# A filter network on half the columns, first weights cast behind the squares, tables through GpSimd's queue

## The chip, the cores and the metric

One NeuronCore of one Trainium2 chip runs the whole kernel. The metric is the time of one execution in device microseconds (us); the kernel before was timed three times: 1154.57, 1156.49 and 1156.57 us, median 1156.49. Engines are named as in the profile: PE (matrix multiply), PEld (its weight loads), DVE (vector), ACT (scalar with function tables), POOL (GpSimd), SP (sync). SP, ACT and POOL also issue DMAs; the instructions of each engine run in the order in which they stand in its queue.

## The reference

An encoder layer on `x` of 1024 rows by 1024 columns, float32. `h` is the RMS norm of `x`, and `proj = h @ w_in` is cut into the inputs of two branches and their gates. The part that matters here is the filter of the Hyena branch, which depends on no row of `x`:

```python
h = rms_norm(x, g_norm[l])
proj = h @ w_in[l]
...
# hyena_filter_spectra: z is (L, 33), a fixed table of times t, cos and -sin
h = jnp.sin(freq_1 * (z @ w_f1 + b_f1))          # 33 -> 64
h = jnp.sin(freq_2 * (h @ w_f2 + b_f2))          # 64 -> 64
k = (h @ w_f3).reshape(L, HY_ORDER, 2, HY_WIDTH) # 64 -> 2 orders x 2 directions x 512
k = k * decay[:, None, None, :]
k_full = jnp.concatenate([k[:, :, 0], k[::-1, :, 1]], axis=0)
return jnp.fft.rfft(k_full.astype(jnp.float32), axis=0)
...
zc = gate * long_conv(zc, k_spec[:, o], hy_bias[l, o])
```

The attention branch, the merge of the two and the output projection follow; the change leaves them as they are.

## The kernel before, in words

Every product in float32 is made of three products of float32r parts: a tile is cast to a high part (ACT), the rest is subtracted (DVE), and PE adds high by high, low by high and high by low. `split` (L138, L139) makes the two parts, `gsplit` (L142, L143) does it with a scale.

**Start.** `load_x` brings `x` in eight tiles of 128 rows, by SP and ACT in turns. `build_hT` works on two groups of four tiles: squares and their sums (ACT, in the first group DVE too), a reciprocal root in twelve tiny DVE instructions (`rsqrt`, L152 to L158), rows scaled on DVE (`xs`, L223), transposes on PE into PSUM (`ptx`, L230), and the two parts of the transposed rows, `hh` on ACT and `hl` on DVE.

**Projection blocks.** `proj_block` loads 128 columns of `w_in` as two `wr` tiles (SP), splits them into `wh` and `wl`, and runs 48 matmuls of 512 columns (`pm`, L567) into two PSUM banks. `fill_g` makes a gate of such a block (ACT, sigmoid) and stores it. `wr` has two buffers: SP issues the next load when DVE has made the `wl` of the tile two before. Eight gate blocks (GEARLY) are written next to the filter stage and fill PE there.

**Filter network.** `filter_loads` brings the table of times `z2` and the two small weights on SP's queue. `z2` holds the 33 features of a time in rows 0 to 32 and those of the mirrored time in rows 64 to 96, for all 1024 times; `wf1` and `wf2` are block diagonal, so one product gives both directions. `filter_mlp` runs each layer on two tiles of 512 columns: three matmuls (`pf`), then `sin_layer` (L254 to L261): scale on DVE (`sx`), two instructions that give the multiple of 2 pi (`sk`), three that subtract it (L258), a clamp, and the sine on ACT. `filter_tables` splits the third layer's weight (`w3h`, `w3l`) and the transform table `ku` (`kuh`, `kul`) on ACT and DVE.

**Spectra.** `filter_spectra` has four rounds (order by half of the channels). In a round, four steps take the third layer's product (`pk`, L348 and L349, two PSUM banks) times the decay (`kk`, L350) into `A` and `B`; the table `dec` of 512 KB for a step comes by SP's queue into one of two buffers, so its load is issued when the step two before has been multiplied. Then `forward` and `leaf_fwd` transform the sums (`pu`, L128) and store the spectra.

Who goes first is decided when the program is built: a scheduler puts the instructions of each engine in one order, with `behind` adding an order without a wait (`after=self.half0` puts the small casts behind the first half of `hh`). On PE the matmuls of projection blocks stand between those of the filter.

The functions that the change touches, with the profile's line numbers:

Of the kernel before, what the change touches and what calls it, by code (L numbers as in the profile page):

```python
# [10 lines left out]
F32 = mybir.dt.float32  # L11
F32R = mybir.dt.float32r
# [29 lines left out]

def _constants():
# [19 lines left out]
    for k in KS[1:]:  # L63
# [24 lines left out]
    return {  # L88
        "sel": sel, "z2": z2, "dec": d2, "ku": ku, "gu": gu, "rt": rt,
        "ident": np.eye(P, dtype=f32),  # L90
    }


class K:
# [106 lines left out]
    def build_hT(self, hp, xp):  # L201
# [5 lines left out]
        xt = self.xt  # L207
        bank = lambda t: self.pp.tile([P, 512], F32, tag=t, bufs={"mm": MMB, "tp": 2, "cv": CVB}[t], name=self.nm("ptx"))
        for g in range(2):
            for i in range(4):  # L210
                tt = 4 * g + i
                sq = xp.tile([P, D], F32, tag="sq", bufs=2, name=self.nm("sq"))
                if i % 2 and g == 0:
                    nc.vector.scalar_tensor_tensor(out=sq, in0=xt[tt], scalar=1.0, in1=xt[tt], op0=ALU.mult, op1=ALU.mult, accum_out=ss[:, tt:tt + 1])
                else:
                    nc.scalar.activation(out=sq, in_=xt[tt], func=AF.Square, accum_out=ss[:, tt:tt + 1])
# [30 lines left out]
    def sin_layer(self, fp, ps, b, fr, cols):  # L247
# [3 lines left out]
        x = fp.tile([P, n], F32, tag="sx", bufs=2, name=self.nm("sx"))  # L251
        k = fp.tile([P, n], F32, tag="sk", bufs=2, name=self.nm("sk"))
# [4 lines left out]
        for c in (6.28125, 0.0019350051879882812, 3.019915981956753e-07):  # L257
# [6 lines left out]
    def filter_loads(self, f1):  # L264
        nc, a = self.nc, self.a
        self.selr = f1.tile([P, P], F32, tag="selr", name="selr")
        nc.sync.dma_start(out=self.selr, in_=a["sel"])
# [4 lines left out]
        self.z2 = f1.tile([P, L], F32, tag="z2", name="z2")  # L272
        nc.sync.dma_start(out=self.z2, in_=a["z2"])

    def filter_mlp(self, fp, f1):
# [22 lines left out]
        for c in range(2):
            sl = slice(c * 512, (c + 1) * 512)
            ps = self.pp.tile([P, 512], F32, tag="cv", bufs=CVB, name=self.nm("pf"))  # L300
            self.mm3(ps, w2h, w2l, h1h[:, sl], h1l[:, sl], True, True)
            x = self.sin_layer(f1, ps, fv[:, 2:3], fv[:, 3:4], 512)
            for d in range(2):
                a_, b_ = slice(64 * d, 64 * d + 64), slice(64 - 64 * d, 128 - 64 * d)
                nc.scalar.copy(out=self.h2[d][a_, sl], in_=x[a_])
                nc.vector.tensor_tensor(out=self.h2[d][b_, sl], in0=x[a_], in1=self.h2[d][a_, sl].bitcast(F32), op=ALU.subtract)

    def filter_tables(self, fp):
        nc, a = self.nc, self.a
        self.kuh = fp.tile([P, 18, P], F32R, tag="kuh", name="kuh")  # L310
        self.kul = fp.tile([P, 18, P], F32R, tag="kul", name="kul")
        with self.pool("fp2") as f2:
            wf3 = f2.tile([P, 2, HY], F32, tag="wf3", name="wf3")
            w3v = a["w_f3"][0].rearrange("k (o d c) -> d k o c", o=2, d=2)
            for d in range(2):
                nc.scalar.dma_start(out=wf3[64 * d:64 * d + 64], in_=w3v[d])
            for d in range(2):
                for s in (slice(0, 64), slice(64, 128)):
                    nc.scalar.copy(out=self.w3h[d][s], in_=wf3[64 * d:64 * d + 64])
                s = slice(64 * d, 64 * d + 64)  # L320
# [944 lines left out]
```

## Time and profile before

| | us |
|---|---|
| median of 3 runs | 1156.49 |
| lowest, highest | 1154.57, 1156.57 |
| the profiled execution's own time | 1155.32 |
| its span in the trace | 1153.4 |
| PE busy | 1099.4 (95%) |
| DVE busy | 893.0 (77%) |
| ACT busy | 589.4 (51%) |
| POOL busy | 107.3 (9%) |

The profiled execution lies 1.2 us below the median and inside the range of the three runs. Matmuls overlap each other in the trace, so PE "busy" means that one is under way. "PEclk" is the granted clock as a share of 2.4 GHz: 1.00 is that, 0.50 is 1.2 GHz. A wait is put down to what ended it.

### The profile page before, as it was taken

Reading aid. Unit: us, or ns where it says so; the run is one execution under the profiler, and the core shown is the slowest. Engines: PE = TensorE matmul, PEld = TensorE weight load, DVE = VectorE, ACT = ScalarE, POOL = GpSimd, SP = SyncE. Lnnn points to the kernel's source line nnn. Section 1 sums busy time; section 2 is a strip of 40 time slices with the busy share of each in tenths; the row PEclk is TensorE's granted clock in tenths of the full one; section 3 lists DMA queues with packets and bytes.
Section 4 is the critical chain, followed back from the end, with each engine's and each line's share of the span. In section 5 each row is a group of like instructions: output and inputs, shape, how many; then the busy total and the mean of one; then the engine's idle time right before and its main releaser. Section 6 shows DMA issues by size and latency. Waiting matters only on the chain.

```text
span 1153.4 us, 15529 instructions
## 1 busy us (share of the span) xinstructions
PE 1099.4 (95%) x5525; PEld 909.7 (79%) x5525; DVE 893.0 (77%) x1631; ACT 589.4 (51%) x1101; POOL 107.3 (9%) x112
## 2 busy tenths in 40 slices
PE   4899999999999999999999999999999999999996
PEld 3678888888888888878887887787888887778874
DVE  6988788698788886778774893789788888478882
ACT  6745555754445434433433852777877776322420
POOL 0000000000000000000000132102200000250353
PEclk9989999999999999999999999899999999999998
DMA  5446444642335334334227557402202001896345
GB/s 212 133 146 198 155 163 174 205 119 65 89 91 147 105 115 128 91 88 127 91 83 233 148 154 248 146 29 74 92 25 77 1 20 50 274 298 217 91 128 182
DMA packets 119221, 150.27 MB, mean 130 GB/s; under 512 B 8548, under 2 KB 82408, under 8 KB 119144
## 3 DMA queue, kind: packets, MB, share of 16 engines
q1 hardware_dynamic: 107688, 120.97, 34.1%
q10 hardware_dynamic: 11456, 28.32, 6.6%
q8 instruction: 43, 0.70, 0.3%
q14 instruction: 34, 0.28, 0.1%
HBM read 101.81 MB, written 47.45 MB: 129 GB/s over the span
## 4 chain that ended last, share of the span: by engine, by line
PE 65%; DVE 14%; DMA 10%; ACT 6%; issue 3%; POOL 1%; SPq 0%; ACTq 0%; POOLq 0%; DVEq 0%
PE pm L567 33%; PE pu L128 8%; PE pt L903 4%; PE pi L128 4%; DMA wor<-in_w_out_dram 3%; PE S L119 2%; PE S L122 2%; PE S L121 2%; ACT pr L889 2%; PE pv L915 2%; PE pv L916 2%; DVE gg L988 1%; DMA out_dram<-xr 1%; DVE mo L139 1%; ACT PTh L138 1%
## 5 line engine op out<-in xcount | busy, mean ns | idle before, releaser
L567 PE MATMUL pm<-hh,wh 128*128 128x512 f32 x656 | 208.6, 393 | 1.8 <-DVE hl L143 0.9
L567 PE MATMUL pm<-hl,wh 128*128 128x512 f32 x656 | 208.9, 393 | 0.0
L567 PE MATMUL pm<-hh,wl 128*128 128x512 f32 x656 | 208.3, 392 | 0.1
L567 PEld LDWEIGHTS pm<-hh,wh 128*128 128x128 f32 x656 | 123.1, 189 | 27.7 <-DVE hl L143 1.1
L567 PEld LDWEIGHTS pm<-hh,wl 128*128 128x128 f32 x656 | 123.2, 188 | 26.0 <-DVE wl L139 0.5
L567 PEld LDWEIGHTS pm<-hl,wh 128*128 128x128 f32 x656 | 123.0, 188 | 25.3
L138 ACT CAST wh<-wr 128x512 fp32r<-128x512 f32 x98 | 60.3, 621 | 158.1 <-PE pm L567 107.7
L138 ACT CAST PTh<-pt 128x512 fp32r<-128x512 f32 x128 | 72.8, 587 | 41.1 <-PE pt L903 39.6
L139 DVE TENSOR_TENSOR PTl<-pt,PTh 128x512 fp32r<-128x512 f32 x128 | 83.8, 682 | 10.8 <-ACT PTh L138 10.2
L887 DVE TENSOR_REDUCE mx<-S 128x1 f32<-128x1024 f32 x64 | 77.9, 1217 | 13.2 <-PE S L122 13.1
L139 DVE TENSOR_TENSOR wl<-wr,wh 128x512 fp32r<-128x512 f32 x95 | 66.8, 708 | 15.7 <-ACT wh L138 15.4
L903 PE MATMUL pt<-ident,pr 128*128 128x128 f32 x512 | 75.9, 278 | 2.4 <-DVE PTl L139 1.4
L889 ACT ACTIVATE pr<-S,mx 128x1024 f32<-128x1024 f32 x64 | 71.8, 1121 | 7.0 <-DVE mx L887 6.6
L903 PEld LDWEIGHTS pt<-ident,pr 128*128 128x128 f32 x512 | 59.3, 142 | 18.2 <-DVE PTl L139 4.7
L915 PE MATMUL pv<-PTh,vc 128*128 128x256 f32 x256 | 69.1, 297 | 0.4 <-DVE at L926 0.4
L916 PE MATMUL pv<-PTl,vc 128*128 128x256 f32 x256 | 67.9, 293 | 0.0
L473 DVE TENSOR_TENSOR t<-pu,kt 128x512 f32<-128x512 f32 x64 | 41.0, 681 | 31.3 <-PE pu L128 30.7
L138 ACT CAST rh<-res 128x512 fp32r<-128x512 f32 x64 | 39.5, 619 | 41.8 <-PE pu L128 20.5
L119 PE MATMUL S<-kh,qh 96*128 96x512 f32 x128 | 54.5, 426 | 2.4 <-ACT pr L889 2.3
L121 PE MATMUL S<-kh,ql 96*128 96x512 f32 x128 | 53.5, 418 | 0.0
L122 PE MATMUL S<-kl,qh 96*128 96x512 f32 x128 | 52.5, 410 | 0.0
L915 PEld LDWEIGHTS pv<-PTh,vc 128*128 128x128 f32 x256 | 48.5, 189 | 4.7 <-DVE at L926 1.9
(285 smaller groups left out, 2391.2 us busy)
## 6 DMA issues: line engine op xcount, KB each, us to landing
wr<-in_w_in_dram SPq DMA_DIRECT2D x82, 256.0 KB, 3.2
wor<-in_w_out_dram SPq DMA_DIRECT2D x36, 256.0 KB, 4.7
dec<-in_dec_dram SPq DMA_DIRECT2D x16, 512.0 KB, 3.6
gT<-ob ACTq DMA_DIRECT2D x16, 512.0 KB, 2.9
gg<-gT SPq DMA_DIRECT2D x16, 512.0 KB, 4.4
kd<-kt ACTq DMA_DIRECT2D x28, 256.0 KB, 2.3
kt<-kd SPq DMA_DIRECT2D x28, 256.0 KB, 2.7
m<-gg ACTq DMA_DIRECT2D x16, 256.0 KB, 4.3
```

The lines of the kernel that those rows point to most:

```text
L119: m = nc.tensor.matmul(out, lhsT=lh, rhs=rh, start=start, stop=False)
L121: nc.tensor.matmul(out, lhsT=ll, rhs=rh, start=False, stop=False)
L122: nc.tensor.matmul(out, lhsT=lh, rhs=rl, start=False, stop=stop)
L128: m = self.nc.tensor.matmul(out, lhsT=x, rhs=y, start=n == 0, stop=n == len(ops) - 1)
L138: self.behind(self.nc.scalar.copy(out=hi, in_=x), after)
L139: (eng or self.nc.vector).tensor_tensor(out=lo, in0=x, in1=hi.bitcast(F32), op=ALU.subtract)
L567: nc.tensor.matmul(ps[c][0:m], lhsT=w[:, i, 0:m], rhs=h[d][:, c * 512:(c + 1) * 512], start=(d == 0 and f == 0), stop=(d == 7 and f == 2))
L887: nc.vector.tensor_reduce(out=mx, in_=ps, axis=AX.X, op=ALU.max, negate=True)
L889: i = nc.scalar.activation(out=pr, in_=ps, func=AF.Exp, bias=mx, accum_out=RS[h // 2][:, qb, h % 2:h % 2 + 1])
L903: nc.tensor.transpose(out=pt[:, i], in_=pr[:, kb * P:(kb + 1) * P], identity=self.ident)
L915: nc.tensor.matmul(pv, lhsT=V[h][:, kb], rhs=hi[:, kb], start=(kb == 0), stop=False)
L916: nc.tensor.matmul(pv, lhsT=V[h][:, kb], rhs=lo[:, kb], start=False, stop=(kb == 7))
```

## The change

- **Network on half the columns.** The table of times has 512 columns: rows 0 to 32 hold the first 512 times, rows 64 to 96 the other 512. Each layer is one tile of 512 columns: three `pf` matmuls and one `sin_layer` in place of two. The mirrored direction is made at the end: `h2` becomes four tiles, and two DVE copies read a tile backwards (`h[:, ::-1]`). The sine's reduction subtracts in two instructions instead of three.
- **Tables come in two parts.** The high and low parts of `z2` and `ku` are made on the host and loaded as float32r; `sel` is loaded as float32r too. The ACT casts and DVE subtractions of `z2`, `ku` and `sel` are gone, and twice the bytes of `ku` are loaded (2.36 MB in all).
- **GpSimd's queue.** The parts of `z2`, `kuh`, `kul`, `sel`, all sixteen `dec` tables and the four bias rows are issued by POOL, in one order. `follow` starts a group of them with a one-element copy: the `z2` parts behind tile 6 of `x`, `kuh`, `kul` and `sel` behind the low part of the second `w3` tile. SP keeps the weights of the projection.
- **Third weight.** `w_f3` is loaded on ACT's queue in four pieces behind `half0`, both directions on all 128 partitions.
- **First block's order.** `gates` replaces `fill_g`: the casts of block 0 stand behind the last of `x`'s squares on ACT, and its subtractions behind the first group's scaled rows on DVE; those of block 1 behind `half0`; the sigmoid of a block is written after the next block's matmuls.
- **Idle transposes.** 36 transposes of raw `x` tiles, into a bank that nobody reads, stand on PE ahead of the first real ones.
- `sq` gets one buffer for ACT and one for DVE in the first group.

```diff
     z2 = np.zeros((P, L // 2), f32)
     z2[:33] = z[:L // 2].T
     z2[64:97] = z[L // 2:].T
...
     for n, x in (("z2", z2), ("ku", ku)):
         t[n + "h"], t[n + "l"] = _parts(x)
...
+        idle = self.pp.tile([P, 512], F32, tag="tp", bufs=2, name="idle")
+        for i in range(4):
+            for j in range(8 if i < 3 else 12):
+                nc.tensor.transpose(out=idle[:, :P], in_=xt[i][:, (j % 8) * P:(j % 8 + 1) * P], identity=self.ident)
...
+    def follow(self, pool, x, moves):
+        nc = self.nc
+        dum = pool.tile([1, 1], F32, tag="fol", bufs=2, name=self.nm("fol"))
+        last = nc.gpsimd.tensor_copy(out=dum, in_=x)
+        for out, in_ in moves:
+            i = nc.gpsimd.dma_start(out=out, in_=in_)
+            self.behind(i, last)
+            last = i
...
+        wf3 = [f1.tile([P, 2, HY], F32, tag=f"wf3{d}", name=f"wf3{d}") for d in range(2)]
+        for d in range(2):
+            for s in range(2):
+                self.behind(nc.scalar.dma_start(out=wf3[d][64 * s:64 * s + 64], in_=w3v[d]), self.half0)
...
+        ps = self.pp.tile([P, L // 2], F32, tag="cv", bufs=CVB, name=self.nm("pf"))
+        self.mm3(ps, w1h, w1l, zh, zl, True, True)
+        x = self.sin_layer(f1, ps, fv[:, 0:1], fv[:, 1:2], L // 2)
+        self.split(x, h1h, h1l)
+        for d in range(2):
+            self.split(wf3[d], self.w3h[d], self.w3l[d], after=self.half0)
+        ps = self.pp.tile([P, L // 2], F32, tag="cv", bufs=CVB, name=self.nm("pf"))
+        self.mm3(ps, w2h, w2l, h1h, h1l, True, True)
+        x = self.sin_layer(f1, ps, fv[:, 2:3], fv[:, 3:4], L // 2)
         for c in range(2):
+            a_, b_ = slice(64 * c, 64 * c + 64), slice(64 - 64 * c, 128 - 64 * c)
+            h, r = self.h2[0, c], self.h2[1, 1 - c]
+            nc.scalar.copy(out=h[a_], in_=x[a_])
+            nc.vector.tensor_tensor(out=h[b_], in0=x[a_], in1=h[a_].bitcast(F32), op=ALU.subtract)
+            nc.vector.tensor_copy(out=r, in_=h[:, ::-1].bitcast(F32))
...
-                    nc.sync.dma_start(out=dec, in_=a["dec"][hf, tp].rearrange("p (d t c) -> p d t c", d=2, t=2))
+                    nc.gpsimd.dma_start(out=dec, in_=a["dec"][hf, tp].rearrange("p (d t c) -> p d t c", d=2, t=2))
+                    if (o, hf, tp) == (0, 0, 1):
+                        self.follow(wk, self.w3l[1][0:1, 0, 0:1].bitcast(F32), ((self.kuh, a["kuh"]), (self.kul, a["kul"]), (self.sel, a["sel"])))
...
+    def gates(self, bs):
+        ps = None
+        for b in bs:
+            new = self.proj_block(3232 + b * P, P, *(((self.squares, self.scaled), (self.half0, None)) + ((None, None),) * 14)[b])
+            if ps is not None:
+                self.gate_out(b - 1, ps)
+            ps = new
+        self.gate_out(bs[-1], ps)
```

How the instructions stand: on DVE, in the first layer of the network. `pf` is a layer's product, `sx` and `sk` its sine's tiles, `wl` a projection weight's low part (`wl_1635` belongs to block 1 before, `wl_1620` and `wl_1650` to block 1 and the next two to block 2 in the change). Before:

```order
L254 TENSOR_SCALAR sx_364<-pf_360,cols 128x512
L139 TENSOR_TENSOR wl_1635<-wr_1632,wh_1634 128x512
L255 TENSOR_SCALAR sk_365<-sx_364 128x512
L254 TENSOR_SCALAR sx_382<-pf_378,cols 128x512
L256 TENSOR_SCALAR sk_365<-sk_365 128x512
L255 TENSOR_SCALAR sk_383<-sx_382 128x512
L258 SCALAR_TENSOR_TENSOR sx_364<-sk_365,sx_364 128x512
L256 TENSOR_SCALAR sk_383<-sk_383 128x512
```

And in the change, from the low part of the third weight on:

```order
L148 TENSOR_TENSOR w3l_384<-wf_390,w3h_382 128x1024
L266 TENSOR_SCALAR sx_410<-pf_406,cols 128x512
L148 TENSOR_TENSOR w3l_385<-wf_391,w3h_383 128x1024
L267 TENSOR_SCALAR sk_411<-sx_410 128x512
L148 TENSOR_TENSOR wl_1620<-wr_1617,wh_1619 128x512
L268 TENSOR_SCALAR sk_411<-sk_411 128x512
L148 TENSOR_TENSOR wl_1650<-wr_1647,wh_1649 128x512
L270 SCALAR_TENSOR_TENSOR sx_410<-sk_411,sx_410 128x512 x2
L272 TENSOR_SCALAR sx_410<-sx_410 128x512
L148 TENSOR_TENSOR wl_1686<-wr_1683,wh_1685 128x512
L148 TENSOR_TENSOR wl_1716<-wr_1713,wh_1715 128x512
L148 TENSOR_TENSOR h1l<-sx_410,h1h 128x512
```

One chain of the sine stands where two stood in turns; the low parts of `w3` now come ahead of block 1's first `wl`, and those of block 2 ahead of `h1l`.

On PE, at the first `pk` of the spectra (third layer; `pm` are projection matmuls: 1630 and 1631 block 1 before, 1681 and 1682 block 2 in the change). Before, `pk` follows the last matmuls of block 1:

```order
L567 MATMUL pm_1630<-hl_154,wh_1664 128x512
L567 MATMUL pm_1631<-hl_154,wh_1664 128x512
L567 MATMUL pm_1630<-hh_146,wl_1665 128x512
L567 MATMUL pm_1631<-hh_146,wl_1665 128x512
L348 MATMUL pk_475<-w3h_340,h_344 128x256
L349 MATMUL pk_475<-w3l_342,h_344 128x256
```

In the change it follows the 33rd matmul of block 2:

```order
L577 MATMUL pm_1681<-hh_148,wl_1716 128x512
L577 MATMUL pm_1682<-hh_148,wl_1716 128x512
L577 MATMUL pm_1681<-hh_149,wh_1715 128x512
L577 MATMUL pm_1682<-hh_149,wh_1715 128x512
L577 MATMUL pm_1681<-hl_157,wh_1715 128x512
L358 MATMUL pk_459<-w3h_382,h_386 128x256
L359 MATMUL pk_459<-w3l_384,h_386 128x256
```

Thirty-three more projection matmuls stand ahead of the third layer.

On the queues that issue `dec`, `bia` (a bias row) and `wr` (projection weights). Before, on SP:

```order
L339 DMA bia_470<-in_hy_bias_dram 1x256
L342 DMA dec_472<-in_dec_dram 128x1024
L342 DMA dec_490<-in_dec_dram 128x1024
L339 DMA bia_744<-in_hy_bias_dram 1x256
L559 DMA wr_1764<-in_w_in_dram 128x4x128
L559 DMA wr_1794<-in_w_in_dram 128x4x128
L342 DMA dec_507<-in_dec_dram 128x1024
```

In the change, on POOL, behind the first two `dec`:

```order
L292 COPY fol_476<-w3l_385 1x1
L294 DMA kuh<-in_kuh_dram 128x2304
L294 DMA kul<-in_kul_dram 128x2304
L294 DMA sel<-in_sel_dram 128x128
L349 DMA dec_496<-in_dec_dram 128x1024
L346 DMA bia_1007<-in_hy_bias_dram 1x16x16
L349 DMA dec_513<-in_dec_dram 128x1024
```

The tables of the transform stand between the second and the third `dec`, and no `wr` stands among them any more. From about the 600th microsecond of the span on, the order on every engine is the same in both kernels.

## Rows read from the trace of the kernel before

**Rows 1.** Windows: busy us (count) by engine, then PEclk, DMA share, GB/s.
```profile
core 0: us, PE busy (x) PEld busy (x) DVE busy (x) ACT busy (x) POOL busy (x), PEclk, DMA share, GB/s
45.00:65.00 20.00, 13.23 (x48) 9.79 (x47) 18.50 (x30) 14.20 (x19) 0.00 (x0) 0.83 0.53 170
65.00:620.00 555.00, 554.61 (x2609) 457.73 (x2608) 439.49 (x869) 254.72 (x504) 1.60 (x24) 1.00 0.41 126
```

**Rows 2.** Windows, the gap and the stretch behind it.
```profile
52.70:58.80 6.10, 0.30 (x2) 0.00 (x0) 6.07 (x9) 5.45 (x8) 0.00 (x0) 0.93 0.36 145
58.80:64.70 5.90, 5.38 (x16) 4.41 (x17) 4.87 (x9) 3.02 (x5) 0.00 (x0) 0.50 0.47 149
```

**Rows 3.** Timeline around the first pk: start, us, engine, line, [idle before <-releaser].
```profile
58.12 2.83 DVE L306 TENSOR_TENSOR h<-sx,h 64x512 fp32r<-64x512 f32 x4
...
58.86 0.58 PE L348 MATMUL pk<-w3h,h 128*128 128x256 f32 x1 [5.86 <-DVE h L306]
```

**Rows 4.** Groups by form, 35 to 62 us, DVE: busy us, mean ns.
```profile
L258 DVE SCALAR_TENSOR_TENSOR sx<-sk,sx 128x512 f32<-128x512 f32 x12 | 7.6, 685 | 0.0
L254 DVE TENSOR_SCALAR sx<-pf,cols 128x512 f32<-128x512 f32 x4 | 3.1, 806 | 0.1
...
L139 DVE TENSOR_TENSOR wl<-wr,wh 128x512 fp32r<-128x512 f32 x4 | 2.7, 688 | 0.4 <-ACT wh L138 0.4
L139 DVE TENSOR_TENSOR kul<-kur,kuh 128x1152 fp32r<-128x1152 f32 x2 | 2.6, 1348 | 0.0
L322 DVE TENSOR_TENSOR w3l<-wf,w3h 64x1024 fp32r<-64x1024 f32 x2 | 2.4, 1215 | 0.0
L255 DVE TENSOR_SCALAR sk<-sx 128x512 f32<-128x512 f32 x4 | 1.6, 420 | 0.0
```

**Rows 5.** Timeline of the start: PE, DVE, ACT's queue.
```profile
15.74 5.52 PE L230 MATMUL ptx<-ident,xs 128*128 128x128 f32 x28 [8.60 <-DVE xs L223]
...
21.36 4.70 DVE L143 SCALAR_TENSOR_TENSOR hl<-ptx,cols,hh 128x512 fp32r<-128x512 f32 x7 [0.48 <-ACT hh L142]
...
28.69 1.47 PE L230 MATMUL ptx<-ident,xs 128*128 128x128 f32 x12
...
30.90 5.35 DVE L143 SCALAR_TENSOR_TENSOR hl<-ptx,cols,hh 128x512 fp32r<-128x512 f32 x8
...
34.65 1.27 ACTq L316 DMA_DIRECT2D wf<-in_w_f_dram  x2
```

**Rows 6.** The chain that ended last: start, us, projection matmuls at full clock.
```profile
74.12 9.09 PE pm L567 x40
```

**Rows 7.** Groups by form, 35 to 62 us, ACT.
```profile
L319 ACT CAST w3h<-wf 64x1024 fp32r<-64x1024 f32 x4 | 4.2, 1051 | 3.0 <-DMA wf<-in_w_f_dram 3.0
...
L683 ACT ACT_TABLE_LOAD x2 | 2.6, 1283 | 0.0
...
L261 ACT ACTIVATE sx<-sx 128x512 f32<-128x512 f32 x4 | 2.4, 626 | 1.1 <-DVE sx L260 1.1
...
L138 ACT CAST wh<-wr 128x512 fp32r<-128x512 f32 x2 | 1.1, 613 | 0.0
```

**Rows 8.** DMA issues of the page: count, KB each, median us to landing.
```profile
wr<-in_w_in_dram SPq DMA_DIRECT2D x82, 256.0 KB, 3.2
```

**Rows 9.** DMA view, 2 to 14 us, while x is loaded.
```profile
DMA packets 1890, 4.66 MB, mean 388 GB/s; under 512 B 204, under 2 KB 831, under 8 KB 1890
```

**Rows 10.** Tile dec, all sixteen loads.
```profile
DMA to landing us min/median/max: 3.5/3.6/6.5
```

**Rows 11.** Timeline of the second round: dec issues, kk of step 3, and first pu.
```profile
104.46 2.73 SPq L342 DMA_DIRECT2D dec<-in_dec_dram  x2
...
108.56 1.27 DVE L350 TENSOR_TENSOR kk<-pk,dec 128x512 f32<-128x512 f32 x2
...
119.72 0.13 DVE L115 COPY dum<-rl 1x1 f32<-1x1 f32 x1
...
119.86 0.28 PE L128 MATMUL pu<-rh,kuh 128*128 128x256 f32 x1
```

More of the change, by code (lines that the diff above doesn't have):

```diff
@@ L87, in _constants @@
     sel[0:64:32, :64] = sel[1:64:32, 64:] = 1.0
[L88 to L91, printed above, removed]
+    t = {"sel": sel, "gu": gu, "dec": d2, "rt": rt, "ident": np.eye(P, dtype=f32)}
+    for n, x in (("z2", z2), ("ku", ku)):
+        t[n + "h"], t[n + "l"] = _parts(x)
+    return t
 class K:
@@ L135, in behind, with split @@
             self.tc.add_manual_dep(i.ins, after.ins.name, mybir.DependencyInfo(mybir.DependencyClass.NoSync, mybir.DependencyReason.DATA), reason="order")
-    def split(self, x, hi, lo, eng=None, after=None):
+    def split(self, x, hi, lo, eng=None, after=None, then=None):
         self.behind(self.nc.scalar.copy(out=hi, in_=x), after)
-        (eng or self.nc.vector).tensor_tensor(out=lo, in0=x, in1=hi.bitcast(F32), op=ALU.subtract)
+        self.behind((eng or self.nc.vector).tensor_tensor(out=lo, in0=x, in1=hi.bitcast(F32), op=ALU.subtract), then)
     def gsplit(self, x, g, hi, lo):
@@ L215, in build_hT @@
                 else:
[L216 removed]
+                    self.squares = nc.scalar.activation(out=sq, in_=xt[tt], func=AF.Square, accum_out=ss[:, tt:tt + 1])
             if g == 0:
@@ L298, in filter_mlp @@
[L298 to L320, printed above, removed]
-                nc.gpsimd.memset(self.w3l[d][64 - 64 * d:128 - 64 * d].bitcast(F32), 0.0)
-                nc.vector.tensor_tensor(out=self.w3l[d][s], in0=wf3[s], in1=self.w3h[d][s].bitcast(F32), op=ALU.subtract)
-            for i in range(2):
-                kur = f2.tile([P, 9, P], F32, tag="kur", bufs=2, name=self.nm("kur"))
-                nc.scalar.dma_start(out=kur, in_=a["ku"][:, 9 * i:9 * i + 9])
-                self.split(kur, self.kuh[:, 9 * i:9 * i + 9], self.kul[:, 9 * i:9 * i + 9])
@@ L549, in conv, with proj_block @@
         return Y
-    def proj_block(self, c0, m=P):
+    def proj_block(self, c0, m=P, after=None, then=None):
         nc, wp = self.nc, self.wp
@@ L561, in proj_block @@
             wl = wp.tile([P, 4, P], F32R, tag="wl", bufs=4, name=self.nm("wl"))
-            self.split(raw[:, :, 0:m], wh[:, :, 0:m], wl[:, :, 0:m])
+            self.split(raw[:, :, 0:m], wh[:, :, 0:m], wl[:, :, 0:m], after=after, then=then)
             for i in range(4):
@@ L1210, in hyena_mla_kernel @@
                 k.fill_z(b)
-            for b in range(GEARLY, 16):
-                k.fill_g(b)
+            k.gates(range(GEARLY, 16))
             k.hyena_tiles(yp)
```

82 lines of the change are left out of this document (39 added, 43 removed).

## The prediction, made before the changed kernel was timed

> **What bounds the kernel now.** I read the windows first, by stage. From 65 to 620 us PE is busy 554.61 of 555.00 us at full clock: nothing there can be gained except by taking matmuls away. Between 45 and 65 us it is busy only 13.23 of 20 us, and the mean clock is 0.83 [rows 1]. Behind the 620th microsecond the order of the instructions does not change, so I count that part as equal. Narrower windows show what the 20 us hold: from 52.7 to 58.8 PE stands still while DVE works 6.07 of 6.10 us, and from 58.8 to 64.7 it works at half clock, 0.50 [rows 2]. The timeline names the wait: the first `pk` came 5.86 us late, released by the subtraction that makes `h2` [rows 3]. So the filter network on DVE ends last in this stage, the projection matmuls in front of it run out, and the pause costs a second time through the clock: after 5.86 us without a matmul the rows show 1.2 GHz for 5.9 us.
>
> What the stage loses: 20.00 - 13.23 = 6.77 us of idle time, and half of the 5.38 us worked at half clock, 2.69. Together 9.46 us.
>
> **The change part by part.**
>
> *Work on PE.* Two layers of two tiles become two layers of one: 6 `pf` matmuls of 512 columns fewer. A full-clock matmul takes 9.09 / 40 = 0.227 us [rows 6]. Gain 1.36. The 36 idle transposes lie in the 8.60 us in which PE waits for the first scaled rows [rows 5]; the wait began at 7.1, and at 0.2 us each they take 7.2 us and are through by 14.3. Cost nothing; without that cover each would cost its own length.
>
> *The start.* The 28 real transposes took 5.52 us, 0.197 each, 12 later ones 1.47, 0.122 each. If the idle ones warm the array, the 22nd ends near 18.4 and `hh` is early; what then ends last is DVE's rsqrt chain, which stood 0.48 us still for `hh` [rows 5]. Gain between 0 and 0.48, I take 0.4. The DVE casts that leave the middle of this stage (`zl`) lay beside transposes that DVE waits for anyway. So the second half of `hl`, which ended at 30.90 + 5.35 = 36.25 [rows 5], ends near 36.0 (0.4 earlier, less part of one `wf` issue, 1.27 / 2 = 0.64, which now stands between two `hh` on ACT).
>
> *New waits behind it.* Three places, worked forward from 36.0.
> (a) Block 1's first cast. ACT does two small casts (0.3 each), two `w3h` of 1.05 and `wh` of 0.61 behind the last `hh` [rows 7], which ends one `hl` before 36.0, at 35.35: 35.35 + 0.6 + 2.1 + 0.6 = 38.7, or 39.4 if the last piece of `w3` lands late. PE has the 24 matmuls of block 0's second half, 16 transposes and three `pf` from 30.25 on: 24 x 0.227 + 16 x 0.122 + 0.68 = 8.1, with small waits 38.8. Loss 0 to 0.6, I take 0.4.
> (b) Block 1's first `wl` stands behind both `w3l`. DVE from `w3h` at 37.0: `w3l` 1.22, `sx` 0.81, `w3l` 1.22, `sk` 0.42, `wl` 0.69 [rows 4]: 41.3. PE has four matmuls that need only `wh`: 39.2 + 0.9 = 40.1. Loss 1.1.
> (c) The second layer's product stands after 31 matmuls of block 1: 41.3 + 27 x 0.227 = 47.4. Its input is behind block 2's casts on ACT: `wr` is issued when block 1's `wl` has freed the buffer, 41.3, and lands 3.2 later [rows 8], 44.5; then `wh`, table load, sine, `wh`, `h1h`: 0.61 + 1.28 + 0.63 + 0.61 + 0.61 = 3.74 [rows 7], 48.3. Loss 0.9.
> Sum of new waits 2.4, none of them near the 5.86 us after which the clock was seen at half.
>
> *Does the old gap close?* The third layer now stands behind 17 more matmuls of block 1, 3 `pf` and 33 of block 2: 48.3 + 53 x 0.227 = 60.3. Behind block 1 (52.8) ACT does a sigmoid, a table load, the sine, a table load, a sigmoid, the cast, about 5.1 together [rows 7], DVE the subtraction (0.69): `h2` at 58.7. The backward copies take 0.42 (like `sk`) to 0.69 (like `wl`) each, and only the second `pk` needs them, 1.4 us later. The gap closes with about 1.5 us to spare. DVE has lost two sine chains, two `kul` of 1.35 and more, over 10 us [rows 4], so it is not late.
>
> *The transform tables.* `kuh` and `kul`, 2.36 MB, are issued when `w3l` is done, near 41, just as SP asks for the `wr` of (c). No row shows a GpSimd load; at 388 GB/s, the rate while `x` was loaded [rows 9], they take 6.1 us. Shared evenly, each `wr` of 0.26 MB takes 0.7 us longer; if `wr` gets nothing until they are through, it lands 4.5 later. Bounds 0 to 4.5, I take 1.0. Their own use is near 80 us, far off. The Trainium skill (DMA: Bandwidth & Descriptors, section Issuing engines are not separate DMA queues) says that DMAs of all three queues interleave on the same 16 engines; by it another queue gives no separate road, which is the even share above, 0.7.
>
> *The decay tables.* In round 2 before, the third step's `dec` was issued at 104.46 and used at 108.56, 4.1 later [rows 11]; from SP such a load took 3.5 to 6.5, median 3.6 [rows 10]. Half a microsecond is left, and another 0.4 between DVE's last word for the first `pu` (119.72 + 0.13) and that `pu`. The order of `pk`, `pm` and `pu` in a round is nearly the same after the change. So a landing that is y longer from GpSimd costs each round y - 0.9. y lies between -0.1 and 2.9 (the slowest SP load): 0 to 8 us over four rounds. Nearest is the median plus the bias row that is now issued ahead on the same queue, y about 1.1: I take 1.0 in all. In the second and later rounds a cast copy, a split less or more on DVE has no weight: `pm` covers it.
> The Trainium skill (SBUF — State Buffer, section SBUF: two separate sides) warns of the opposite: GpSimd cannot write its descriptors while DVE runs a copy or scalar operation in its two-port mode. By it the `z2` loads could wait for a row scaling and `kuh` for an `sk` (0.42 here), while a round holds almost only two-input operations; it adds nothing to the sum, and no row here shows it.
>
> *Sum.* 9.46 - 2.4 + 1.36 + 0.4 = 8.8 faster; less 1.0 and 1.0, 6.8. The profiled execution took 1155.32, so 1148.5; it lies 1.2 below the median of the three runs and among them, and I say 1149.
>
> **The rivals.**
>
> *No new wait counts.* (a) to (c) are estimates of about a microsecond each, and weights may land sooner. Then all of 9.46 + 1.36 + 0.4 = 11.2 is gained: 1144.1. Against it: the order on ACT and DVE puts four `w3` instructions ahead of block 1.
>
> *The wait moves to the second layer.* `wr` is starved by the tables: (c) grows by 4.5 to 5.4 us, PE stands as long as it did before `pk`, and the clock drops again for up to 2.7. 1155.3 - 8.8 + 1.0 + 7.2 = 1154.7, no change that can be told. For it: both loads start within a microsecond, and `h1h` stands behind two `wh` on ACT. Against it: while `x` was loaded on two queues at 388 GB/s, both moved.
>
> *Slower: the rounds wait for GpSimd's tables.* One load per queue turn, each behind the `kk` of two steps before, four rounds. From a landing of 6.5 us on (y = 2.9) the rounds cost 4 x 2.0 = 8 and the gain is gone; at 8 us (y = 4.4) they cost 14: 1155.3 - 7.8 + 14 = 1161.5. For it: the slack of 0.9 is small. Against it: an SP load reached 6.5 only once the other queues were full.
>
> *The change does not do what it says* would be a `pk` that still waits for `h2`. The margin of 1.5 us covers one table load; a chain 4 us late would give back 2.5: 1151.
>
> **How the numbers follow.** About 0.2%, 2.3 us, is what a measurement of this kernel can tell from no change; against 1156.5 that puts "faster" below 1154.2 and "slower" above 1158.8. Forecast with its neighbours (1145.5 to 1152.5, the late `pk` among them) 0.60; no new wait 0.12; the moved wait 0.17, of which a third still under 1154.2; the rounds 0.11, of which 0.08 above 1158.8. Faster 0.60 + 0.12 + 0.06 = 0.78, slower 0.08, with 0.01 for what I do not see 0.09, the rest 0.13. The range leaves out 0.05 below and about 0.12 above: 1143.5 to 1156.
>
> **What would show it.** In the profile of the changed kernel: no wait of `pk` for `h2` and PEclk 1.00 from 22 us to 620; transposes at 0.12 us from the first on and `hl` starting near 20.9; PE waits of about 1 us for `wl` of block 1 near 40 and for `h1h` near 48; PE full from 50 to 620; `dec` landing in 3.5 to 5 us. Wrong would be: a PE pause of 4 us or more between 40 and 60 with a clock of 0.50 behind it (moved wait), or `kk` waiting for `dec` and PE for `kk` or `rl` in every round (the tables).

## The result, and the profile after

Median of four runs 1167.43 us (1166.79 to 1168.01), against 1155.53 for the kernel before; ratio 1.0103, 95% interval 1.0088 to 1.0118. The change makes the kernel 12 us slower, where 1149 was forecast, 7 faster. The profiled execution took 1167.39 us, its span is 1165.6.

Windows of the changed kernel: the two of [rows 1], the new gap, the stretch behind it, and the start (columns as in rows 1).

```profile
45.00:65.00 20.00, 12.11 (x43) 9.43 (x42) 6.94 (x13) 5.04 (x8) 0.00 (x0) 0.74 0.61 196
65.00:620.00 555.00, 550.96 (x2581) 453.37 (x2581) 439.51 (x851) 257.15 (x506) 10.04 (x40) 1.00 0.40 123
49.30:57.20 7.90, 0.03 (x1) 0.00 (x0) 1.21 (x2) 3.56 (x5) 0.00 (x0) 0.69 0.70 221
57.20:62.70 5.50, 5.48 (x13) 4.32 (x14) 4.27 (x8) 0.62 (x1) 0.00 (x0) 0.52 0.40 98
21.00:25.00 4.00, 3.11 (x7) 2.51 (x8) 3.99 (x7) 1.83 (x4) 0.00 (x0) 0.57 0.38 113
```

DVE, which was full in the old gap [rows 2], works 1.21 of 7.90 us in the new one; DMA is busy instead (0.70 of the time, as a mean over its 16 engines). PE stands, then works 5.5 us at half clock, and at the start too there is a stretch near 0.5. From 65 to 620 PE is idle 4.0 us; it was 0.4.

The timelines show what the new gap waits for (start, us, engine or queue, line, operation, [idle before <-releaser]):

```profile
42.24 0.55 POOL L294 DMA_DIRECT2D kuh<-in_kuh_dram  x1
42.80 0.55 POOL L294 DMA_DIRECT2D kul<-in_kul_dram  x1
...
42.89 1.31 SPq L569 DMA_DIRECT2D wr<-in_w_in_dram  x2
...
53.58 0.62 ACT L147 CAST wh<-wr 128x512 fp32r<-128x512 f32 x1 [10.54 <-DMA wr<-in_w_in_dram]
54.22 1.28 ACT L273 ACT_TABLE_LOAD   x1
55.51 0.63 ACT L273 ACTIVATE sx<-sx 128x512 f32<-128x512 f32 x1
...
57.22 0.79 PE L128 MATMUL pf<-h1h,w2h 128*128 128x512 f32 x1 [7.89 <-ACT h1h L147]
...
71.96 0.39 PE L358 MATMUL pk<-w3h,h 128*128 128x256 f32 x1
```

POOL issues both tables at 42.2 and 42.8, SP the two `wr` of block 2 from 42.9 on. Only at 53.5 has the first `wr` landed. Its cast stands on ACT ahead of the sine's table load, the sine and `h1h`, so the second layer's `pf` is 7.89 us late. The first `pk` waits for nothing: the old gap [rows 3] is closed. The landing times of `wr` from 40 to 60 us, of `kul` and of the sixteen `dec` (first, second, third line):

```profile
DMA to landing us min/median/max: 2.8/2.9/10.6
...
DMA to landing us min/median/max: 9.8/9.8/9.8
...
DMA to landing us min/median/max: 3.8/4.7/7.1
```

`kul` landed at 42.8 + 9.8 = 52.6, the first `wr` just behind it, 10.6 us after its issue where 3.2 is usual [rows 8]. `dec` takes 4.7, against 3.6 [rows 10].

What the three queues moved from 48 to 51 us, while all were at work (packets, MB, share of the DMA engines' time; q0 is GpSimd's queue, q1 SP's, and q10 ACT's, which stores a gate, `gT`, of 512 KB issued at 43.1):

```profile
q0 software_dynamic: 92, 0.84, 68.6%
q10 hardware_dynamic: 86, 0.35, 28.5%
q1 hardware_dynamic: 88, 0.05, 7.5%
```

Each queue moved about as many packets as the others, but a packet is one row here: 9216 bytes of a table, 4096 of the store, 512 of a `wr`. So `wr` got 0.05 of 1.24 MB. From 43 to 47 us only q0 moved anything: SP's first packet came at 47.2, 4.3 us after its issue, where the `wr` issued at 54.95 had its first after 1.0. What held it there is not shown.

Where the kernels drift apart (start of the first instruction of each kind on PE, from the timelines; in brackets how many projection matmuls stand ahead of it on PE):

| | before | after | e1 | e5 | e9 |
|---|---|---|---|---|---|
| first `pm` | 22.17 | 21.89 | 21.80 | 22.61 | 21.72 |
| second layer's `pf` | 46.37 | 57.22 | 48.80 | 51.50 | 49.08 |
| first `pk` | 58.86 (96) | 71.96 (129) | 61.08 (129) | 63.77 (129) | 61.34 (129) |
| first `pu` | 83.04 (171) | 90.79 (192) | 90.42 (214) | 82.60 (192) | 80.12 (192) |
| first `pi` | 243.88 (601) | 252.48 (608) | 249.77 (608) | 244.46 (608) | 240.46 (608) |
| first `pq` | 625.43 (1831) | 633.99 (1831) | 630.82 (1831) | 626.24 (1831) | 619.94 (1831) |
| span | 1153.4 | 1165.6 | 1160.7 | 1158.1 | 1150.2 |

Matmuls that one kernel has already done are not lost, so each lag is lessened by 0.227 us [rows 6] for every projection matmul more. The changed kernel is then behind by 13.10 - 33 x 0.227 = 5.6 us at the first `pk`, 3.0 at the first `pu` (the kernel before ran at half clock in between, [rows 2]), 7.0 at `pi`, 8.6 at `pq`.

### The profile page after: what moved, and what is told of

Same layout as the page of the kernel before. It is cut to its first block, busy times and chain, and to the rows that moved or that the text cites. A ratio compares the mean times of both kernels' runs of the same rounds, so it can differ in the third digit from the quotient of the medians.

```text
span 1165.6 us, 15587 instructions
## 1 busy us (share of the span) xinstructions
PE 1105.9 (95%) x5555; PEld 914.1 (78%) x5555; DVE 881.6 (76%) x1610; ACT 580.3 (50%) x1089; POOL 120.3 (10%) x137
## 4 chain that ended last, share of the span: by engine, by line
PE 65%; DVE 13%; DMA 10%; ACT 7%; issue 3%; POOL 1%; SPq 0%; ACTq 0%; POOLq 0%; DVEq 0%
PE pm L577 30%; PE pu L137 7%; PE pt L922 4%; PE pi L137 4%; DMA wor<-in_w_out_dram 2%; PE S L128 2%; PE S L130 2%; PE S L131 2%; ACT pr L908 2%; PE pv L934 2%; PE pv L935 2%; PE pmo L130 1%; PE pmo L128 1%; PE pmo L131 1%; PE pth L877 1%
## 5 line engine op out<-in xcount | busy, mean ns | idle before, releaser
L577 PE MATMUL pm<-hl,wh 128*128 128x512 f32 x656 | 211.6, 395 | 0.0
L131 PE MATMUL S<-kl,qh 96*128 96x512 f32 x128 | 52.6, 411 | 0.0
```

The costliest lines, as they stand in the source:

```text
L131: nc.tensor.matmul(out, lhsT=lh, rhs=rl, start=False, stop=stop)
L577: nc.tensor.matmul(ps[c][0:m], lhsT=w[:, i, 0:m], rhs=h[d][:, c * 512:(c + 1) * 512], start=(d == 0 and f == 0), stop=(d == 7 and f == 2))
```

## The experiments

Ratios are to the kernel before, timed on the same chip with each call. Single runs lie up to 6 us from the median of their kernel, so ratios carry the verdicts, and a trace shows the mechanism of one execution.

**e1: the tables later.**

```diff
-self.follow(wk, self.w3l[1][0:1, 0, 0:1].bitcast(F32), ((self.kuh, ...
+self.follow(wk, self.h2[1, 0][0:1, 0:1].bitcast(F32), ((self.kuh, ...
```

> The changed kernel, with the loads of kuh, kul and sel released by the last copy of h2 instead of by w3l. Theory (starved load): the 2.36 MB of the two tables, issued at 42.2 and 42.8, hold back the wr of block 2, issued at 42.9 and landed at 53.5; its cast stands on ACT ahead of the first sine, so PE stood 7.89 us and then ran 5.5 us at half clock. With the tables gone from there that wr lands about 3 us after its issue, h1h is made near 49, and 9 to 11 us come back: 1156 to 1159 us. Rival (order): ACT's queue, with a wh cast and a table load ahead of the sine, is late by itself, whoever transfers: 1165 to 1169 us. Rival (moved again): the tables now starve a wr near 62 to 70 us and a third to a half of the gain is lost there: 1160 to 1164 us.

1167.48 us, ratio 1.0094 (1.0061 to 1.0127): no gain in the median. The profiled execution is the fastest of the four (1162.44; the others 1167.12 to 1168.55). Its trace is not that of the rival "order": the pause at the second layer fell to 0.67 us, and a new one stood 30 us later:

```profile
48.80 0.50 PE L128 MATMUL pf<-h1h,w2h 128*128 128x512 f32 x1 [0.67 <-ACT h1h L147]
...
63.12 0.55 POOL L294 DMA_DIRECT2D kuh<-in_kuh_dram  x1 [0.28 <-issue]
...
67.41 11.51 SPq L569 DMA_DIRECT2D wr<-in_w_in_dram  x3
...
77.18 0.62 ACT L147 CAST wh<-wr 128x512 fp32r<-128x512 f32 x1 [8.14 <-DMA wr<-in_w_in_dram]
77.83 0.69 DVE L148 TENSOR_TENSOR wl<-wr,wh 128x512 fp32r<-128x512 f32 x1 [8.64 <-ACT wh L147]
78.44 1.28 DVE L360 TENSOR_TENSOR kk<-pk,dec 128x512 f32<-128x512 f32 x2
79.27 0.55 PE L358 MATMUL pk<-w3h,h 128*128 128x256 f32 x1 [3.86 <-DVE kk L360]
```

The first `pk` came 10.9 us earlier, the first `pu` only 0.4; but 22 projection matmuls more were done by then, worth 5.0 us, so this execution was 5.4 ahead there, and 4.9 at its end. Now a `wr` asked for at 67.4 waits for the tables until 77.2, its cast holds ACT, its `wl` holds DVE, the `kk` behind it holds PE. The load starves the `wr` that it meets here too: "moved again", with half of the gain lost in this execution. Why the other three took 5 us more is not shown.

**e2: no idle transposes.** (The loop over `nc.tensor.transpose(out=idle...)` and its tile are gone.)

```diff
-nc.tensor.transpose(out=idle[:, :P], in_=xt[i][:, (j % 8) * P:(j % 8 + 1) * P], identity=self.ident)
```

> The changed kernel without the 36 idle transposes. Theory: they make the 28 transposes of group 0 faster (0.117 us each against 0.197) but then PE stands 2.59 us for hl, the granted clock falls to 0.50 from 21 to 25 us and the first 7 pm matmuls take 0.425 us each instead of 0.23 (1.4 us); without them the clock does not fall there, and since hl waits for rsqrt and two wl casts on DVE anyway, the first pm comes at most 0.5 us later: 1 us comes back, 1165.5 to 1167 us. Rival: the faster transposes are worth their 2.3 us, since hl follows them: 1168.5 to 1170 us.

1164.78 us, ratio 1.0077 (1.0053 to 1.0101): by the ratios 3.0 us less than the changed kernel, more than the theory's 1; the intervals just overlap. The first `pm` came at 22.23, 0.34 later than with them.

**e3: decay tables by SP.**

```diff
-nc.gpsimd.dma_start(out=bia, ...   -nc.gpsimd.dma_start(out=dec, ...
+nc.sync.dma_start(out=bia, ...     +nc.sync.dma_start(out=dec, ...
```

> The changed kernel with the decay tables (dec) and bia issued by SP again; PE's, DVE's and ACT's orders stay word for word. Theory: of the 5 us that PE lost between 75 and 620 us and before did not lose, half belongs to dec landing late (4.7 us median by GpSimd's queue against 3.6) and DVE's kk waiting for it (3.0 us): 1164 to 1166 us, and PE's waits between 150 and 260 us shrink. Rival: those waits come from the other order of gates and casts, and dec costs nothing: 1166.5 to 1168.5 us. Rival: two dec loads of 512 KB on SP ahead of the wr of block 2 delay that wr by another 1 to 3 us: 1169 to 1171 us.

1166.43 us, ratio 1.0096 (1.0069 to 1.0122): 0.8 less, inside the uncertainty. DVE's waits for `dec` in the rounds fell from 3.0 us to 0.4 in the trace, though a `dec` by SP's queue landed no sooner in this kernel (median 5.2, by GpSimd's 4.7). The other waits before `pi` stayed.

**e4: gates in the old order.**

```diff
-            if ps is not None:
-                self.gate_out(b - 1, ps)
-            ps = new
-        self.gate_out(bs[-1], ps)
+            self.gate_out(b, new)
```

> The changed kernel with each gate written right behind its own projection block, as in the kernel before, instead of behind the next block's; casts of blocks 0 and 1 stay where the change puts them. Theory: the later place of the gates on ACT makes the two waits of 1.25 and 0.5 us and the fall of the clock near 250 us (3 us in all): 1163 to 1165.5 us. Rival: the gates' place is no cause, the waits come from what was late before: 1166 to 1169 us.

1164.58 us, ratio 1.0084 (1.0050 to 1.0118). The median is one that the theory gave, but the interval reaches to 1169, so the times do not decide. The waits that the theory put down to the gates are still in the trace (of an execution of 1169.03): `ptt` 0.68 and 0.52, `pi` 1.28 and 0.29 us, and the clock falls behind them. The gates are not their cause. This trace settles one thing more: ACT's store of `gT` had landed by 44.1 here, before `wr` moved, and still a `wr` took 10.0 us to land and the second layer's `pf` came 7.3 late. The tables alone do it.

**e5: the tables early**, with the orders of PE, DVE, ACT and SP unchanged (on GpSimd's queue the tables now stand ahead of the first two `dec`).

```diff
-self.follow(wk, self.w3l[1][0:1, 0, 0:1].bitcast(F32), ((self.kuh, ...
+self.follow(f1, self.hh[0][0:1, 0:1].bitcast(F32), ((self.kuh, ...      # in filter_mlp
```

> The changed kernel with kuh, kul and sel released by the first hh tile (near 19 us) instead of by w3l (42 us); PE's, DVE's, ACT's and SP's orders stay word for word, so only the time of the transfer moves. Theory (starved load, moved with the tables in e1): between 19 and 30 us no wr is close to its use (block 1 is cast at 39), so the wait of 7.9 us at the second layer and the half clock behind it go and nothing takes their place: the second layer's pf begins near 49, the first pk near 61, the first pu near 80 to 82 instead of 90.8, and the time is 1156 to 1159 us. Rival (the rounds bound it): the time from the first pk to the first pu grows again as in e1 without any late transfer: first pu near 88, 1164 to 1167 us. Rival: the wr of block 1 is now starved and the first pf or the second half of block 1 is late by 3 to 5 us: 1160 to 1163 us.

1159.38 us, ratio 1.0026 (1.0010 to 1.0042): by the ratios 9 us less, for these loads at another time. Issued at 20.6, the tables meet no `wr` that is needed soon; the pause is 1.01 us and the first `pu` comes at 82.60, 8.2 earlier. PE's timeline:

```profile
42.36 0.73 PE L575 MATMUL pm<-hh,wh 128*128 128x512 f32 x2 [1.96 <-ACT wh L147]
...
51.50 0.50 PE L128 MATMUL pf<-h1h,w2h 128*128 128x512 f32 x1 [1.01 <-ACT h1h L147]
```

The window of the stage, PE at full clock:

```profile
45.00:65.00 20.00, 18.99 (x85) 15.00 (x83) 10.26 (x18) 12.85 (x17) 0.00 (x0) 1.00 0.46 132
```

The time is just above what the theory gave. A smaller pause was new, 1.96 us at block 1's first matmul; e6 shows its cause.

**e6: e5 and e3 together.**

```diff
+nc.sync.dma_start(out=dec, ...                                          # e3
+self.follow(f1, self.hh[0][0:1, 0:1].bitcast(F32), ((self.kuh, ...      # e5
```

> As e5, and the decay tables and bia by SP as in e3. Theory: the two gains add, e3's being about 2 us between the first pu and the first pi: 1154 to 1157 us. Rival: with the rounds 10 us earlier the dec loads on SP hold back wr loads behind them and nothing is gained over e5: 1157 to 1160 us.

1156.88 us, ratio 1.0019 (1.0003 to 1.0035): by the ratios 0.8 us less than e5, again too little to tell, and less than the 2 expected. On ACT:

```profile
32.00 0.54 ACTq L310 DMA_DIRECT2D wf<-in_w_f_dram  x1
...
39.79 1.04 ACT L147 CAST w3h<-wf 128x1024 fp32r<-128x1024 f32 x1 [3.51 <-DMA wf<-in_w_f_dram]
40.74 1.14 ACT L147 CAST wh<-wr 128x512 fp32r<-128x512 f32 x2
```

The last piece of the third weight, issued at 32.0, landed near 39.8, and block 1's cast stands behind it. The tables had landed at 31.8; what it moved beside were the first two `dec` (issued at 28.1 and 28.8, landed after 8.8 and 10.6 us). In e9, with the tables through by 26.0, the pieces of the weight took 3.8 us and these `dec` 5.2 and 6.4.

**e7: e6 without the idle transposes.**

```diff
+nc.sync.dma_start(out=dec, ...                                          # e3
+self.follow(f1, self.hh[0][0:1, 0:1].bitcast(F32), ((self.kuh, ...      # e5
-nc.tensor.transpose(out=idle[:, :P], ...                                # e2
```

> As e6, and without the idle transposes. Theory: the idle transposes bring nothing, since hl waits for DVE (first pm at 22.2 without and 21.9 with them) and they leave PE to stand before the first pm: 0 to 2 us less than e6, 1153 to 1157 us, and not slower than the kernel before. Rival: the 0.4 us of the first pm is all there is: 0.4 us more than e6.

1152.41 us, ratio 0.9979 (0.9960 to 0.9998): 4.5 us less than e6, more than the 0 to 2 expected, and for the first time below the kernel before.

**e8: the tables in smaller pieces**, at the place of the change.

```diff
-((self.kuh, a["kuh"]), (self.kul, a["kul"]), (self.sel, a["sel"]))
+[(t[:, i:i + 3], a[n][:, i:i + 3]) for t, n in ((self.kuh, "kuh"), (self.kul, "kul")) for i in range(0, 18, 3)] + [(self.sel, a["sel"])]
```

> The changed kernel with kuh and kul loaded where it loads them, but as six pieces each (196 KB, rows of 1536 bytes instead of 9216). Theory (shares go by rows): the wr of block 2, with rows of 512 bytes, gets a share of the transfers in proportion to the length of its rows against those of the other queue; with rows six times shorter it lands 3 to 6 us earlier than 53.5, and PE's wait of 7.9 us falls to 2 to 5: 1161 to 1165 us. Rival (bytes ahead): whatever was issued first goes first, and the wr lands when the tables have: 1166 to 1168 us.

1162.62 us, ratio 1.0061 (1.0037 to 1.0085): 5 us less. PE's timeline has a pause of 1.70 us, and a second one for `h2`:

```profile
49.99 0.50 PE L128 MATMUL pf<-h1h,w2h 128*128 128x512 f32 x1 [1.70 <-ACT h1h L147]
...
64.22 0.38 PE L358 MATMUL pk<-w3h,h 128*128 128x256 f32 x1 [1.91 <-DVE h L332]
```

The landing of `wr` from 40 to 60 us:

```profile
DMA to landing us min/median/max: 2.8/4.9/6.5
```

So not "bytes ahead": the same bytes at the same place hold `wr` back less when they come in pieces. Two things differ: the rows are shorter (1536 bytes), and twelve issues spread the tables from 41.2 to 50.1. For the row's length speak the equal counts of packets in the changed kernel. In e8's trace the counts are not equal: from 51 to 52 us the tables moved 107 packets and `wr` 430, from 52 to 53 it was 278 and 19. So this run does not tell the two apart.

**e9: e7 with the tables still earlier.**

```diff
+            if g == 0:                                                  # in build_hT, behind the xs
+                self.follow(xp, xs[3][0:1, 0:1], ((self.kuh, ...
```

> As e7 (tables early, dec and bia by SP, no idle transposes), with the tables released by the last xs of group 0 (near 17.5 us) instead of by the first hh (21.3 in e7). In e7 kul landed at 30.0, and the third layer's weight, issued at 32.5 beside 1 MB of dec, took 5.1 us. Theory: from 17 to 20 us the transfers stood still (2 to 6 GB/s); 3.5 us earlier the tables are gone by 27 and ACT's waits for the weight (0.9 us) and for wr (2.2 us) shrink: 0 to 1.5 us less than e7, 1150.5 to 1153 us, ratio to the kernel before 0.9965 to 0.9985. Rival: the tables now hold back a wr of block 0 or the rest of x and the first pm comes after 22.5: 1153 to 1156 us.

1151.67 us, ratio 0.9964 (0.9951 to 0.9977): the fastest, 4.2 us below the kernel before. The windows of [rows 1]: the stage is nearly full, at full clock.

```profile
45.00:65.00 20.00, 18.63 (x88) 14.75 (x87) 10.77 (x19) 12.41 (x16) 0.00 (x0) 1.00 0.32 89
65.00:620.00 555.00, 551.50 (x2587) 453.53 (x2586) 441.75 (x873) 254.74 (x505) 1.60 (x24) 1.00 0.41 128
```

All `wr` from 40 to 60 us land in 2.8 us now, and the second layer waits little:

```profile
49.08 0.50 PE L128 MATMUL pf<-h1h,w2h 128*128 128x512 f32 x1 [1.28 <-ACT h1h L147]
```

What PE waits for between 200 and 260 us (engine, line, waited for, us in total, times, longest), in e9 and then in the kernel before:

```profile
PE pi L137 <- ACT ph L147: 1.3, 1, 1.3
PE ptt L617 <- DVE acc L606: 0.8, 2, 0.7
PE ptt L617 <- DVE dum L124: 0.6, 1, 0.6
PE pi L137 <- DVE pl L148: 0.3, 1, 0.3
```

```profile
PE ptt L611 <- DVE acc L600: 0.4, 2, 0.2
```

3.0 us against 0.4. The two waits of `pi` stand in the traces of the changed kernel, of e1 to e10, e13 and e14, with 0.3 and 1.2 or 1.3 us.

**e10: e9 with the idle transposes; e11: the kernel before with them; e12: e9 with the casts of blocks 0 and 1 free.**

```diff
+nc.tensor.transpose(out=idle[:, :P], ...                                # e10, e11
-((self.squares, self.scaled), (self.half0, None)) + ((None, None),) * 14
+((None, None),) * 16                                                    # e12
```

> As e9, with the idle transposes again. Theory: they cost what e2 against the changed kernel (2.6 us) and e7 against e6 (4.5 us) show, at the start and in what follows from it: 2 to 4 us more than e9. Rival: those differences came from which transfer was late in each run (the third layer's weight landed 7.7 us after its issue in e6, 5.1 in e7), not from the transposes; with the tables out of the way e10 equals e9 within 1 us, or is 0.4 us faster, as the first pm is 0.4 us earlier.

> The kernel before with the 36 idle transposes and nothing else of the change; DVE's, ACT's and SP's orders stay word for word. Theory: PE is warm for the 28 transposes of group 0 (0.117 us each instead of 0.197), the first pm comes 0.3 to 1 us earlier, and where the granted clock falls before the first pm 1.4 us are lost again: 1153.5 to 1156.5 us, ratio 0.9995 to 1.0015. Rival (they pay): DVE has no wl in the way here in the order of this kernel, the first pm comes 2 us earlier and the time falls by 1 to 2 us. Rival (they cost): 2 to 4 us more than the kernel before, as in the pairs of the changed kernel.

> As e9, with the casts of gate blocks 0 and 1 free of the order that the change gives them (behind the squares and the xs; behind the first half of hh), so that the scheduler places them. Theory: the fixed places cost the wait for wl of block 1 (0.9 us near 42) and bring 0.3 us at the first pm: within 1 us of e9. Rival: without them the first pm waits for its weights, or the casts stand ahead of squares and hh on ACT, and 1 to 3 us are lost.

e10: 1156.05 us, ratio 0.9998 (0.9985 to 1.0011), 3.9 us more than e9 by the ratios. e11: 1158.96, ratio 1.0024 (1.0013 to 1.0034): the idle transposes alone make the old kernel 2.8 us slower, although its first `pm` came 0.53 earlier; in its trace it is 0.3 behind at the first `pq` and 3.1 at the end. Both are the "they cost" side. e12: 1152.58, ratio 0.9971 (0.9960 to 0.9982), within 1 us of e9: the fixed places of the first casts are worth nothing that can be measured. But PE's order differs with them, and in e12's trace PE has one kind of wait from 200 to 260 us, and none of `pi`:

```profile
PE ptt L617 <- DVE acc L606: 1.2, 2, 0.8
```

**e13 and e14: is it the warm start or the PSUM tile?** The idle tile takes one of the two buffers of its tag and so swaps the banks of all later tiles of that tag.

```diff
+            if i % 2 == 0:                                              # e13: 36 transposes, two tiles
+                idle = self.pp.tile([P, 512], F32, tag="tp", bufs=2, name=self.nm("idle"))
+        nc.tensor.transpose(out=idle[:, :P], in_=xt[0][:, 0:P], identity=self.ident)   # e14: one tile, one transpose
```

> As e10, with the 36 idle transposes written into two tiles of tag tp in turn instead of one, so that every later tile of that tag stands in the bank that it has without them (e9). Theory (banks): e10's 4.4 us over e9 come from the swapped banks; this one is like e9, 1150.5 to 1153 us, ratio 0.995 to 0.998. Rival (warm start): the transposes themselves cost it, by the clock that falls while PE stands before the first pm and by what follows; this one is like e10, 1154.5 to 1157 us, ratio 0.9985 to 1.001.

> As e10, with a single idle transpose instead of 36, so that the tile of tag tp is taken (banks as in e10) but PE is not warm at the first ptx. Theory (banks): like e10, 1154.5 to 1157 us, ratio 0.9985 to 1.001. Rival (warm start): like e9, 1150.5 to 1153 us, ratio 0.995 to 0.998.

e13: 1156.33 us, ratio 1.0007 (0.9991 to 1.0024), like e10. e14: 1151.79, ratio 0.9968 (0.9956 to 0.9980), like e9. It is the 36 transposes, not the banks. e13's timeline of PE, and its windows of the transposes and of the first matmuls:

```profile
16.01 3.28 PE L245 MATMUL ptx<-ident,xs 128*128 128x128 f32 x28 [2.32 <-DVE xs L234]
21.87 0.66 PE L578 MATMUL pm<-hh,wh 128*128 128x512 f32 x1 [2.59 <-DVE hl L152]
```

```profile
16.00:19.30 3.30, 3.28 (x28) 3.04 (x28) 3.20 (x10) 2.24 (x6) 1.29 (x4) 1.00 0.22 61
21.70:25.60 3.90, 3.73 (x9) 2.97 (x10) 3.90 (x7) 1.13 (x2) 0.00 (x0) 0.56 1.07 422
```

The same of e14:

```profile
15.67 5.72 PE L242 MATMUL ptx<-ident,xs 128*128 128x128 f32 x28 [8.53 <-DVE xs L231]
22.19 0.50 PE L575 MATMUL pm<-hh,wh 128*128 128x512 f32 x1 [0.80 <-DVE hl L152]
```

```profile
16.00:19.30 3.30, 3.30 (x17) 3.30 (x16) 3.20 (x10) 1.24 (x4) 1.63 (x4) 1.00 0.32 61
21.70:25.60 3.90, 3.41 (x17) 2.83 (x17) 3.90 (x7) 3.12 (x6) 0.00 (x0) 1.00 1.02 396
```

The 1.00 of e14's first window is no reading: the record of the clock in its trace begins at 20.7 us (in e13's at 11.8), and a view counts the time ahead of it as full. The transposes of e14 start 0.21 us apart until 20.6 and 0.11 apart behind it, those of e13 0.11 apart throughout. The warm transposes are 2.4 us faster, the first `pm` only 0.3 earlier, because `hl` waits for DVE in either case. PE stands 2.59 us instead of 0.80, and the granted clock is 0.56 over the first matmuls: 3.73 x 0.44 = 1.6 us. That is less than half of the cost, and the fall did not come there each time: the traces of e1, e5, e8 and e11 have the 2.6 us pause and full clock behind it, and in e3, e4 and e6 the clock fell earlier, at 17 us, so that the transposes took 4.94 us and PE stood 0.93 before the first `pm`. Over all runs the mean granted clock is 0.989 in e10 and e13 and 0.992 in e9 and e14; over some 1100 us of busy PE that is 3 us, most of the 4. Part of it may be 3.4 us at half clock between 624 and 634 us, which the traces of e6, e10 and e13 have and those of e7, e9 and e14 do not. Why a warm start would bring that stays open.

## Why the prediction was wrong, step by step

- **What bounds the stage: right.** The `pk` pause closed, as worked out, and e9 has 1.37 us idle from 45 to 65 in place of 6.77, with the clock at 1.00.
- **The transform tables: the step that failed.** The prediction took 1.0 us for the sharing, in bounds of 0 to 4.5, and 0.9 for wait (c). Measured: 7.89 us of pause and half of 5.5 at half clock, 10.6 in all. Two errors made the size. The upper bound supposed that the tables are through in 6.1 us; `kul` took 9.8 from its issue. (How 4.5 follows from 6.1 is not worked out there; tables through at 47.1 and the usual 3.2 behind them would have made it 5.8; measured were 10.6 - 3.2 = 7.4.) And the even share of bytes was taken for the likely case, where first `wr` moved nothing for 4.3 us, and then the share was even in packets: 88 against 92, which is 0.05 MB against 0.84. e1, e5 and e8 show from three sides that the tables do it: another time moves the pause or removes it, smaller pieces shorten it. In e9, without the tables there, wait (c) is 1.28 us, near the 0.9 worked out. The sentence from the Trainium skill (DMA: Bandwidth & Descriptors, section Issuing engines are not separate DMA queues) holds in that the queues share the engines; an even share of bytes was my reading, and the trace does not agree with it (10.6 us against 3.2).
- **Its rival had the mechanism and not the price.** "The wait moves to the second layer" was given 0.17 and 7.2 us; place, cause and half clock were right.
- **Idle transposes "cost nothing": wrong**, by 3.0 to 4.6 us in four pairs (e2, e7 against e6, e10 against e9, e13 against e14) and 2.8 on the old kernel. They lie in a pause, as said; what was left out is the pause that they open behind the transposes. It accounts for less than half of their cost; the rest is open.
- **The start, 0.4 us:** the first `pm` came 0.28 earlier; DVE's chain was the bound, as said.
- **Waits (a) and (b):** (a) did not show; (b), 1.1, measured 0.91.
- **Decay tables, 1.0 us:** e3 and e6 gave 0.8 each, a right size within what can be measured. The longer landing was as worked out, 4.7 against 3.6 + 1.1; that it is the queue's doing is not shown, since SP's took 5.2 in e3. Of the slack of 0.9 the second part, 0.4, does not follow from its row: 119.72 + 0.13 is 119.85, and that `pu` started at 119.86. Without it the term would have been 1.6 us larger (four rounds), which e3 and e6 do not show.
- **Counted as equal, and not:** from the first `pu` to the first `pi` the changed kernel lost 4.0 us more than the kernel before, e9 2.7 (the table, less 14 matmuls). Most of it is the waits shown under e9. Neither the gates' order (e4) nor `dec` (e3) makes those of `pi`. With the casts of blocks 0 and 1 free (e12) they are gone, so they hang on the order that these places bring; yet e12 lost 1.8 us over the same stretch (first `pu` at 81.49 behind 193 projection matmuls, first `pi` at 246.63 behind 634) and is no faster. And behind the first `pq`, where the order is the same, the profiled runs of the changed kernel and of every experiment took 0.9 to 7.2 us longer than that of the kernel before (the changed kernel 3.6, e9 2.3). Part of that is scatter between runs; no experiment was aimed at it.
- **The sum.** By the ratios: tables 9, idle transposes 4, `dec` 1, so 14 lost, where 2 were put down. Without the three, 8.4 was worked out for the rest (9.46 - 2.4 + 1.36). In e9's trace 5.5 of it are there at the first `pq` (the 2.7 between `pu` and `pi` are missing), 3.2 at the end; by the ratio 4.2.

## What to carry to other kernels

A big load has a price at the moment when it runs, however far off its own use is: look for the stretch in which no other load is urgent (here 17 to 20 us, when transfers stood at 1 GB/s in the changed kernel), and follow what a late landing holds up on an engine's queue, since a cast in front of a chain makes the chain late. Count the packets of competing queues too and not only their bytes: here the load with the short rows got the small share. In these runs work that only kept an engine warm did not pay: another engine set the moment of what followed, and a pause opened. When a removed wait gives nothing (e1), look for it again further down before dropping the theory.

## What was not expected of the hardware

- Two loads of 1.18 MB by GpSimd's queue held a 256 KB load of SP's queue, issued 0.1 us after the second, to 10.6 us, against 2.9 for its neighbours (e1: 9.8). The same bytes in twelve pieces: at most 6.5. While three queues ran side by side they moved about as many packets each (92, 86 and 88 in 3 us), of 9216, 4096 and 512 bytes.
- 28 transposes of 128 columns took 3.28 us behind 36 others and 5.72 behind a pause of 8.5 us (e13, e14). In e14 they start 0.21 us apart until the record of the clock begins, at 20.7, and 0.11 apart behind it; a view prints 1.00 for the time without a record. Where the record shows a fall over them (e3, e4, e6: 0.65 to 0.70 from 16.0 to 19.3) they took 4.94.
- Behind a pause of 2.59 us the granted clock fell (0.56 to 0.65 from 21.7 to 25.6) in the traces of the changed kernel, e10 and e13 and stayed at 1.00 in those of e1, e5, e8 and e11.
